# Two attention layers on one core: both value products take their low pass from v's high part alone, placed between transposes of the next probabilities

## The chip, the cores and the metric

The kernel runs on one core of a Trainium2 chip. The metric is device time in microseconds of one execution; of the kernel before there are three runs, with a median of 2325.73 us (2324.55 to 2328.28).

## The reference, cut to what matters

Two layers of gated attention run one after the other over a prompt of 2048 tokens and a sample of 64 tokens (with cached keys and values), model width 1024, 16 heads of 64. Both layers follow the same form:

```
p = rms_norm(x) @ w_in                  # q, k, v, gate
q, k = rms_norm per head
s = q k^T / 8 + bias ; p = softmax(s)   # layer A with a sink per head
o = p v                                 # the value product
y = x + (o * silu(gate)) @ w_out
```

Layer A attends to its own chunk of 64 frames and two before it, with 2 key heads for 16 query heads; layer B to its own chunk and eight before it, each head with its own keys and values.

## The kernel before, in words

**Numbers in two parts.** Operands of products are kept as a high part (rounded to fp32r) and a low part (the rest). A projection tile is made of 8 steps over the model width, each of three products of 512 columns: high by high (L481), high by low (L482), low by high (L483). The value product is made of pairs: `vt`, 128 rows of keys by 128 columns, is the stationary operand, and its columns are v's high part (0 to 63) beside v's low part (64 to 127). The moving operand is the transposed probabilities, first their high part `ph` (or `hi`), then their low part `pl` (or `lo`). The output O has 128 rows in PSUM: 0 to 63 belong to v's high part, 64 to 127 to v's low part; `finish_pairs` (L976 to L985) adds the two halves (two ACT copies L981, two DVE additions L983), multiplies by the gate (POOL, L984) and stores (SP's queue, L985). Every product has a weight load of its own, also where two in a row have the same `vt`.

**Transposes.** The probabilities come out with queries on rows. `transpose` (L597) takes a block of 128 keys as the stationary operand and streams the identity. `split_to` then casts the result from PSUM to the high part (ACT, L569) and subtracts it for the low part (DVE, L570).

**Who sets the order.** On TensorE (PE) the order is written out by hand (`manual_schedule`); ACT, DVE, POOL and the DMA queues are ordered by the framework's own scheduler. The attention steps are mixed with "filler": projection tiles of later units and, after them, the output projections. `filler.to(mark)` puts out projection products until a mark is reached; the marks count projection columns alone.

**Layer A** (`layer_a`, `pipeline` from L941 on) works on items: 4 groups of 4 heads times 17 token tiles (16 of 128 prompt tokens, one of the 64 sample tokens), 68 items. Step i does the scores of item i, filler to 0.3 of the step, `values` of item i-1 (8 transposes, 4 for each of two blocks of keys), filler, `turned` (transposes of queries and of the gate G) at 0.8, and at 0.95 `outputs` of item i-1 (two pairs of 512 columns). The first tile of each group has one block of keys, and the sample item has one block of 128 keys and one of 64.

**Layer B** (`layer_b`, `pipeline` from L1199 on) works on 8 pairs of heads; each goes over 8 units of 256 tokens and the sample unit, which stands between the 7th and the 8th. A step handles one tile and one head: scores, filler, `values` of the step before (up to 5 transposes), then, where a head of a unit has all its tiles transposed, `outputs` of that head one step later, filler. A full output is 6 pairs: 4 of 256 columns and 2 of 128 (L1188 high, L1189 low). For the second head, two transposes of the gate (tile G) stand at the head of `outputs`. The sample unit has 64 query rows: its transposes read 64 rows, its products stream 64 columns, and its third block has 64 keys, so 64 rows of `vt`. `gt`, the transposed gate, has one buffer (L969 to L974).

Of the kernel before, what the change touches and what calls it, by code (L numbers as in the profile page):

```python
# [15 lines left out]
P = 128  # L16
# [35 lines left out]
def hybrid_encoder_kernel(  # L52
# [608 lines left out]
    def layer_a():  # L661
# [243 lines left out]
                op=ALU.mult,  # L905
            )

        def values(it):
            qd = it.qd
            tt, t0, n = it.tile  # L910
            ph = t("ph", [P, 6, 256], 2, F32R)
            pl = t("pl", [P, 6, 256], 2, F32R)
            hi, lo = [], []
            for c, (vt, kn) in enumerate(it.vts):
                PT = psum_a("sa", 512, 4)
                for h in range(4):
                    transpose(PT[:kn, h * n : (h + 1) * n], it.pe[h // 2][:n, h % 2, c * P : c * P + kn])
                hi.append(ph[:kn, 2 * c : 2 * c + 2, :].rearrange("p a b -> p (a b)")[:, : 4 * n])
                lo.append(pl[:kn, 2 * c : 2 * c + 2, :].rearrange("p a b -> p (a b)")[:, : 4 * n])
                bg.anchor(*split_to(hi[c], lo[c], PT[:kn, : 4 * n]))  # L920
            it.hi, it.lo = hi, lo

        def outputs(it):
            qd = it.qd
            tt, t0, n = it.tile
            hi, lo = it.hi, it.lo
            O = psum("o", 512, 1)
            m = len(it.vts)
            for c, (vt, kn) in enumerate(it.vts):
                nc.tensor.matmul(O[:, : 4 * n], vt, hi[c], start=c == 0, stop=False)  # L930
                nc.tensor.matmul(O[:, : 4 * n], vt, lo[c], start=False, stop=c == m - 1)
            finish_pairs(
                O[:, : 4 * n].rearrange("p (j e s) -> p j e s", j=2, e=2),
                it.gt,
                n,
                og[0][:, 2 * qd : 2 * qd + 2, tt * P : tt * P + n],
            )
            key = 0, it.unit[0]
            finished[key] = finished.get(key, 0) + 1

        def pipeline():  # L941
            N = len(items)
            for i in range(-3, N + 1):
                c0 = filler.done
                end = c0 + 5.2
                if i + 3 < N:
                    end = max(items[i + 3].mark, c0 + AVG_A)
                filler.attending = i >= 0
                if 0 <= i < N:
                    scores(items[i])  # L950
                    bg.share(AL, AP_)
                filler.to(c0 + 0.3 * (end - c0))
                if 0 <= i - 1:
                    values(items[i - 1])
                    bg.share(AL, AP_)
                if 0 <= i + 2 < N and items[i + 2].qd == 0:
                    filler.to(c0 + 0.6 * (end - c0))
                    keys(items[i + 2])
                filler.to(c0 + 0.8 * (end - c0))
                turned(items[i + 2] if 0 <= i + 2 < N else None, items[i - 1] if 0 <= i - 1 else None)  # L960
                filler.to(c0 + 0.95 * (end - c0))
                if 0 <= i - 1:
                    outputs(items[i - 1])
                filler.to(end)
                assert i + 3 >= N or items[i + 3].ready

# [21 lines left out]
    def layer_b():  # L988
# [143 lines left out]
                        op=ALU.mult,  # L1132
                    )

        def values(it, i, h):
            u, T, tiles = it.unit
            last = u == NU
            tt, t0, n = tiles[i]
            if i == 0:
                it.ph[h] = t("ph", [P, 6, 256], 2, F32R)  # L1140
                it.pl[h] = t("pl", [P, 6, 256], 2, F32R)
            if last:
                sizes, kb = [P, P, TS], 0
            else:
                kt0 = max(tt - 4, 0)
                sizes, kb = [P] * (tt - kt0 + 1), kt0 - it.base
            PT = psum_b("sb", 1024, 2)
            PTv = PT.rearrange("p (c x) -> p c x", x=P)
            for c, kn in enumerate(sizes):
                transpose(PTv[:kn, c, :n], it.p[i, h][:n, c * P : c * P + kn])  # L1150
            full = sum(kn == P for kn in sizes)
            groups = [(0, full, P)]
            if last:
                groups.append((2, 1, TS))
            for c, m, kn in groups:
                bg.anchor(*split_to(
                    it.ph[h][:kn, kb + c : kb + c + m, t0 : t0 + n],
                    it.pl[h][:kn, kb + c : kb + c + m, t0 : t0 + n],
                    PTv[:kn, c : c + m, :n],
                ))  # L1160
            it.sizes = sizes

        def outputs(it, h):
            u, T, tiles = it.unit
            last = u == NU
            n = tiles[0][2]
            sizes = it.sizes
            if h == 0:
                it.O = psum("o", 512, 1)
            else:  # L1170
                GT = psum("tp", 512, 1)
                for e, (_, t0, _) in enumerate(tiles):
                    transpose(GT[:, t0 : t0 + n], it.G[:n, e * P : (e + 1) * P])
                gt = gate_t(GT[:, :T].rearrange("p (j s) -> p j s", j=1), T)
            mm = []
            if last:
                for c, kn in enumerate(sizes):
                    mm.append((VS[:kn, c, h], c, kn, 0, TS))
            else:
                ta, tb = tiles[0][0], tiles[1][0]  # L1180
                for kt in range(max(tb - 4, 0), ta + 1):
                    mm.append((VT[:, kt, h], kt - it.base, P, 0, UT))
                if ta >= 4:
                    mm.append((VT[:, ta - 4, h], ta - 4 - it.base, P, 0, P))
                mm.append((VT[:, tb, h], tb - it.base, P, P, UT))
            for x, (vt, c, kn, q0, q1_) in enumerate(mm):
                dst = it.O[:, h * T + q0 : h * T + q1_]
                nc.tensor.matmul(dst, vt, it.ph[h][:kn, c, q0:q1_], start=x == 0, stop=False)  # L1188
                nc.tensor.matmul(dst, vt, it.pl[h][:kn, c, q0:q1_], start=False, stop=x == len(mm) - 1)  # L1189
            if h == 1:  # L1190
                finish_pairs(
                    it.O[:, : 2 * T].rearrange("p (j e s) -> p j e s", j=1, e=2),
                    gt,
                    T,
                    og[1][:, it.hp : it.hp + 1, u * UT : u * UT + T],
                )
                finished[1, u] = finished.get((1, u), 0) + 1

        def pipeline():  # L1199
# [9 lines left out]
            for x, it in enumerate(its):  # L1209
                heads = [(i, h) for h in range(2) for i in range(len(it.unit[2]))]  # L1210
                c0 = filler.done
                end, near = c0 + (PACE_B if len(heads) == 4 else PACE_S) * len(heads), 1e9
                if x + 2 < len(its):
                    near = its[x + 2].mark
                    if len(its[x + 1].unit[2]) + len(its[x + 2].unit[2]) < 4:
                        near += MORE
                    end = max(its[x + 2].mark, min(end, its[x + 3].mark - 1.0 if x + 3 < len(its) else end))

                def goal(s):
                    filler.to(c0 + min((end - c0) * s / (2 * len(heads)), (near - c0) * s / NS))  # L1220

                for y, (i, h) in enumerate(heads):
                    scores(it, i, h)
                    bg.share(BL, BP_)
                    goal(2 * y + 1)
                    nxt = None
                    if prev is not None:
                        values(*prev)
                        bg.share(BL, BP_)
                        if prev[1] == len(prev[0].unit[2]) - 1:  # L1230
                            nxt = prev[0], prev[2]
                    prev = it, i, h
                    if pend is not None:
                        outputs(*pend)
                    pend = nxt
                    goal(2 * y + 2)
                    if y == (QY if len(heads) == 4 else QS) and x + 1 < len(its):
                        queries(its[x + 1])
                        near = 1e9
                assert x + 2 >= len(its) or its[x + 2].ready  # L1240
            values(*prev)
            filler.to(filler.done + 2.6)
            if pend is not None:
                outputs(*pend)
            filler.to(filler.done + 2.6)
            outputs(prev[0], prev[2])

        return pipeline

# [175 lines left out]
```

## Time and profile before

| | before |
|---|---|
| median of 3 runs | 2325.73 us (2324.55 to 2328.28) |
| span of the profiled execution, first to last instruction | 2323.8 us |
| median less this span | 1.9 us |
| PE (matmul) busy | 2269.6 us, 98% |
| PE weight loads busy | 1985.2 us, 85% |
| DVE, ACT, POOL busy | 1547.3, 1432.7, 847.6 us |
| mean granted TensorE clock | 0.998 of full speed |

The profiled execution's time is told as its span; what lies around the span is taken as the difference to the median, 1.9 us. PE's busy time is the union of matmul records whose ends are modelled (a product's record goes on while the next one starts), so costs are read from the distance between starts. A weight load's record starts when the load begins, which can be as soon as the product before it has begun to stream; so the start of a load also marks the start of the product before it. A row's form, such as 128\*64 128x256, is rows and columns of the stationary operand and the moving operand's rows by columns.

### The profile page before, as it was taken

To read this page: it belongs to the slowest core of one execution; us is meant where nothing else is said; L and a number is where in the kernel's file an instruction comes from. 1 tells how busy PE (TensorE), PEld (TensorE's weight loads), DVE (VectorE), ACT (ScalarE), POOL (GpSimd) and SP (SyncE) were. 2 spreads that over 40 slices of the span, in tenths; PEclk is the share of its full clock that TensorE was granted. 3 is DMA by queue.
4 is the path that set the end of the run, shared out by engine and by line. 5 is a ranking of instruction groups with operands and counts; after the bars stand their busy time and mean duration, and the time that the engine had idled before them with its cause. 6 is when DMAs were issued, how large, how long until landed. Compare 5 with 4: busy or idle time off the path is not lost.

```text
span 2323.8 us, 42433 instructions
## 1 busy us (share of the span) xinstructions
PE 2269.6 (98%) x13981; PEld 1985.2 (85%) x13981; DVE 1547.3 (67%) x5214; ACT 1432.7 (62%) x3644; POOL 847.6 (36%) x1194
## 2 busy tenths in 40 slices
PE   8899999999999998999999999999999999999999
PEld 7787888888889997878888888888888888888999
DVE  7679988887782228876766767767667677676211
ACT  7778777777772236765665656656656566566321
POOL 5554533333254446432222222222222222224443
PEclk9999999999999999999999999999999999999999
DMA  8846446754446776453444533534435435433664
GB/s 256 263 146 207 162 144 195 229 167 162 134 126 204 226 216 219 145 186 126 158 142 128 161 127 114 178 126 152 143 123 163 134 103 177 131 126 106 189 186 148
DMA packets 232126, 379.37 MB, mean 163 GB/s; under 512 B 24721, under 2 KB 163361, under 8 KB 231873
## 3 DMA queue, kind: packets, MB, share of 16 engines
q1 hardware_dynamic: 231904, 376.65, 51.3%
q8 instruction: 110, 1.80, 0.3%
q14 instruction: 112, 0.91, 0.1%
HBM read 296.13 MB, written 82.08 MB: 163 GB/s over the span
## 4 chain that ended last, share of the span: by engine, by line
PE 77%; DVE 10%; ACT 5%; DMA 5%; issue 2%; POOL 1%; SPq 0%; POOLq 0%; ACTq 0%; DVEq 0%
PE pj L481 13%; PE pj L483 12%; PE pj L482 12%; PE pj L1283 5%; PE pj L1284 5%; PE pj L1285 5%; PE sb L597 5%; PE o L1189 3%; PE o L1188 3%; PE tp L597 3%; PE sb L1110 3%; PE sb L1111 3%; PE sa L597 2%; DVE sq L524 1%; DVE p L1114 1%
## 5 line engine op out<-in xcount | busy, mean ns | idle before, releaser
L481 PE MATMUL pj<-wh,xx 128*128 128x512 f32 (+1 forms) x1648 | 668.7, 406 | 15.2 <-DVE ms L433 7.2
L483 PE MATMUL pj<-wh,xx 128*128 128x512 f32 (+1 forms) x1648 | 638.1, 387 | 0.0
L482 PE MATMUL pj<-wl,xx 128*128 128x512 f32 (+1 forms) x1648 | 635.0, 385 | 0.0
L483 PEld LDWEIGHTS pj<-wh,xx 128*128 128x128 f32 x1648 | 310.4, 188 | 67.3
L481 PEld LDWEIGHTS pj<-wh,xx 128*128 128x128 f32 x1648 | 311.9, 189 | 56.9 <-ACT pb L504 6.5
L386 POOL TENSOR_TENSOR xx<-xraw,xx 128x528 fp32r<-128x528 f32 (+1 forms) x200 | 265.6, 1344 | 218.2 <-ACT xx L385 212.0
L482 PEld LDWEIGHTS pj<-wl,xx 128*128 128x128 f32 x1648 | 312.5, 190 | 37.7
L528 POOL TENSOR_TENSOR f<-f,mhalf 128x4 f32<-128x4 f32 (+3 forms) x221 | 227.9, 1031 | 228.7 <-DVE f L524 216.9
L1118 ACT ACTIVATE p<-p,nm 128x640 f32<-128x640 f32 (+5 forms) x272 | 204.4, 751 | 167.2 <-DVE nm L1114 165.1
L1283 PE MATMUL pj<-xx,wh 128*128 128x264 f32 x1024 | 293.3, 286 | 0.1
L1284 PE MATMUL pj<-xx,wh 128*128 128x264 f32 x1024 | 291.3, 284 | 0.0
L1285 PE MATMUL pj<-xx,wl 128*128 128x264 f32 x1024 | 289.8, 283 | 0.0
L1114 DVE CUSTOM_DVE_ANT_0 p<-sb,BT 128x640 f32<-128x640 f32 (+5 forms) x272 | 196.7, 723 | 119.6 <-PE sb L1111 116.2
L570 DVE TENSOR_TENSOR pl<-sb,ph 128x640 fp32r<-128x640 f32 (+5 forms) x288 | 196.8, 683 | 116.1 <-ACT ph L569 113.7
L385 ACT CAST xx<-xraw 128x528 fp32r<-128x528 f32 (+1 forms) x200 | 123.4, 626 | 220.3 <-PE pj L1285 131.9
L984 POOL TENSOR_TENSOR o<-gt,o 128x256 f32<-128x256 f32 (+2 forms) x140 | 107.4, 767 | 371.3 <-issue 149.0
L569 ACT CAST ph<-sb 128x640 fp32r<-128x640 f32 (+5 forms) x288 | 167.1, 580 | 122.4 <-PE sb L597 114.0
L1288 DVE TENSOR_TENSOR res<-pj,res 128x264 f32<-128x264 f32 x128 | 55.1, 431 | 246.5 <-PE pj L1285 230.7
L1283 PEld LDWEIGHTS pj<-xx,wh 128*128 128x128 f32 x1024 | 192.7, 188 | 0.8 <-DVE res L1288 0.3
L1285 PEld LDWEIGHTS pj<-xx,wl 128*128 128x128 f32 x1024 | 192.6, 188 | 0.0
L1284 PEld LDWEIGHTS pj<-xx,wh 128*128 128x128 f32 x1024 | 192.4, 188 | 0.2
L524 DVE CUSTOM_DVE_ANT_0 sq<-pa 128x64 f32<-128x64 f32 (+1 forms) x850 | 170.2, 253 | 22.1 <-ACT pa L504 20.0
(189 smaller groups left out, 4810.5 us busy)
## 6 DMA issues: line engine op xcount, KB each, us to landing
xx<-xsb SPq DMA_DIRECT2D x224, 512.0 KB, 4.1
xx<-xsa SPq DMA_DIRECT2D x88, 512.0 KB, 4.8
xraw<-oga SPq DMA_DIRECT2D x64, 264.0 KB, 3.4
xraw<-ogb SPq DMA_DIRECT2D x64, 264.0 KB, 3.3
xsa<-xx SPq DMA_DIRECT2D x32, 512.0 KB, 4.0
wraw<-in_w_in_b_dram SPq DMA_DIRECT2D x64, 256.0 KB, 3.4
xsb<-xx SPq DMA_DIRECT2D x32, 512.0 KB, 3.8
xraw<-in_x_dram SPq DMA_DIRECT2D x40, 256.0 KB, 4.1
```

Source lines behind the costliest of these rows:

```text
L386: nc.gpsimd.tensor_tensor(xl, rv, xh.bitcast(F32), op=ALU.subtract)
L481: nc.tensor.matmul(ps[:n, :C], xh, wh, start=k == 0, stop=False)
L482: nc.tensor.matmul(ps[:n, :C], xh, wl, start=False, stop=False)
L483: nc.tensor.matmul(ps[:n, :C], xl, wh, start=False, stop=k == KC - 1)
L528: nc.gpsimd.tensor_tensor(fv, fv, mhalf[:n, :H], op=ALU.pow)
L570: b = nc.vector.tensor_tensor(dst_lo, src, dst_hi.bitcast(F32), op=ALU.subtract)
L597: nc.tensor.transpose(out, in_, ident[:n, :n])
L1114: mi = nc.vector.tensor_tensor_reduce(out=p[:n, :nk], in0=S[:n, o : o + nk], in1=bias[:n, b0 : b0 + nk], op0=ALU.add, op1=ALU.min, scale=1 ...
L1118: ex = nc.scalar.activation(p[:n, :nk], p[:n, :nk], AF.Exp, scale=-1.0, bias=nmh, accum_out=it.sm[:n, 2 * i + h : 2 * i + h + 1],)
L1283: nc.tensor.matmul(ps[:, :OT], wh, oh, start=k == 0, stop=False)
L1284: nc.tensor.matmul(ps[:, :OT], wh, ol, start=False, stop=False)
L1285: nc.tensor.matmul(ps[:, :OT], wl, oh, start=False, stop=k == KC - 1)
```

## The change

`outputs` becomes a generator. It first issues the high product of the first block, then hands a list of low products to its caller, and after that issues the other high products and `finish_pairs`. The low products use the stationary columns 0 to 63 alone (v's high part; blocks of 64 keys keep all columns), so that the product of p's low part with v's low part is left out. `values` takes this list and puts one low product behind each transpose, the rest behind the last. In layer A the low products are cut in two of 256 columns, and `outputs` of item i-2 now stands around `values` of item i-1 at 0.3 of step i; before, it stood at 0.95 of step i-1. In layer B the step stays the same, but `outputs` starts ahead of `values` (with the transposes of G first).

```diff
-        def values(it):
+        def values(it, lows=()):
+            lows = list(lows)
...
                 for h in range(4):
                     transpose(PT[:kn, h * n : (h + 1) * n], it.pe[h // 2][:n, h % 2, c * P : c * P + kn])
+                    if lows:
+                        lows.pop(0)()
...
+            for low in lows:
+                low()
 
         def outputs(it):
...
-            for c, (vt, kn) in enumerate(it.vts):
-                nc.tensor.matmul(O[:, : 4 * n], vt, hi[c], start=c == 0, stop=False)
-                nc.tensor.matmul(O[:, : 4 * n], vt, lo[c], start=False, stop=c == m - 1)
+
+            def high(c):
+                vt, kn = it.vts[c]
+                nc.tensor.matmul(O[:, : 4 * n], vt, hi[c], start=c == 0, stop=c == m - 1 > 0)
+
+            def low(c, q):
+                vt, kn = it.vts[c]
+                M = HD if kn == P and m > 1 else P
+                nc.tensor.matmul(O[:M, q], vt[:, :M], lo[c][:, q], start=False, stop=m == 1)
+
+            high(0)
+            parts = [slice(0, 2 * n), slice(2 * n, 4 * n)] if m > 1 else [slice(0, 4 * n)]
+            yield [lambda c=c, q=q: low(c, q) for c in range(m) for q in parts]
+            for c in range(1, m):
+                high(c)
             finish_pairs(
...
                 filler.to(c0 + 0.3 * (end - c0))
+                out = lows = ()
+                if 0 <= i - 2:
+                    out = outputs(items[i - 2])
+                    lows = next(out)
                 if 0 <= i - 1:
-                    values(items[i - 1])
+                    values(items[i - 1], lows)
+                    for _ in out:
+                        pass
                     bg.share(AL, AP_)
...
                 filler.to(c0 + 0.95 * (end - c0))
-                if 0 <= i - 1:
-                    outputs(items[i - 1])
+                if i == N:
+                    out = outputs(items[i - 1])
+                    for low in next(out):
+                        low()
+                    for _ in out:
+                        pass
...
-        def values(it, i, h):
+        def values(it, i, h, lows=()):
+            lows = list(lows)
...
             for c, kn in enumerate(sizes):
                 transpose(PTv[:kn, c, :n], it.p[i, h][:n, c * P : c * P + kn])
+                if lows:
+                    lows.pop(0)()
...
+            for low in lows:
+                low()
 
         def outputs(it, h):
...
-            for x, (vt, c, kn, q0, q1_) in enumerate(mm):
-                dst = it.O[:, h * T + q0 : h * T + q1_]
-                nc.tensor.matmul(dst, vt, it.ph[h][:kn, c, q0:q1_], start=x == 0, stop=False)
-                nc.tensor.matmul(dst, vt, it.pl[h][:kn, c, q0:q1_], start=False, stop=x == len(mm) - 1)
+            def high(x):
+                vt, c, kn, q0, q1_ = mm[x]
+                nc.tensor.matmul(
+                    it.O[:, h * T + q0 : h * T + q1_], vt, it.ph[h][:kn, c, q0:q1_],
+                    start=x == 0, stop=x == len(mm) - 1,
+                )
+
+            def low(x):
+                vt, c, kn, q0, q1_ = mm[x]
+                M = HD if kn == P else P
+                nc.tensor.matmul(
+                    it.O[:M, h * T + q0 : h * T + q1_], vt[:, :M], it.pl[h][:kn, c, q0:q1_],
+                    start=False, stop=False,
+                )
+
+            high(0)
+            yield [lambda x=x: low(x) for x in range(len(mm))]
+            for x in range(1, len(mm)):
+                high(x)
             if h == 1:
                 finish_pairs(
...
                     nxt = None
+                    if pend is not None:
+                        out = outputs(*pend)
+                        lows = next(out)
+                    else:
+                        out, lows = (), ()
                     if prev is not None:
-                        values(*prev)
+                        values(*prev, lows)
+                        for _ in out:
+                            pass
                         bg.share(BL, BP_)
                         if prev[1] == len(prev[0].unit[2]) - 1:
                             nxt = prev[0], prev[2]
                     prev = it, i, h
-                    if pend is not None:
-                        outputs(*pend)
                     pend = nxt
```

At the end of layer B the last two outputs are issued whole, their low products one behind the other.

## Rows read from the trace of the kernel before

**Rows 1.** Page, part 1, then busy time by stage: layer A, layer B.
```profile
PE 2269.6 (98%) x13981; PEld 1985.2 (85%) x13981; DVE 1547.3 (67%) x5214; ACT 1432.7 (62%) x3644; POOL 847.6 (36%) x1194
...
50.00:720.00 670.00, 652.20 (x3781) 551.88 (x3780) 538.65 (x1953) 504.34 (x1395) 286.66 (x468) 1.00 0.57 179
904.00:2171.00 1267.00, 1248.26 (x7415) 1076.78 (x7415) 887.08 (x2958) 800.40 (x2006) 381.14 (x569) 1.00 0.45 142
```

**Rows 2.** Waits of PE: for what; us in total, times, longest us.
```profile
PE o L931 <- DVE pl L570: 5.9, 11, 1.2
...
PE o L1189 <- DVE pl L570: 2.5, 7, 1.0
...
PE tp L597 <- DVE KB L1071: 1.9, 2, 1.4
```

**Rows 3.** Timeline, layer A: one item's output, its last operation, the next output.
```profile
500.90 0.40 PE L930 MATMUL o<-ph,VT 128*128 128x512 f32 x1
...
501.13 0.39 PE L931 MATMUL o<-pl,VT 128*128 128x512 f32 x1
...
504.93 0.74 POOL L984 TENSOR_TENSOR o<-gt,o 128x256 f32<-128x256 f32 x1 [3.40 <-ACT p L894]
...
509.35 0.39 PE L930 MATMUL o<-ph,VT 128*128 128x512 f32 x1
```

**Rows 4.** Timeline of weight loads in one full output of layer B.
```profile
1501.42 0.19 PEld L1188 LDWEIGHTS o<-ph,VT 128*128 128x128 f32 x1
1501.54 0.19 PEld L1189 LDWEIGHTS o<-pl,VT 128*128 128x128 f32 x1
...
1501.89 0.19 PEld L1188 LDWEIGHTS o<-ph,VT 128*128 128x128 f32 x1
1502.00 0.19 PEld L1189 LDWEIGHTS o<-pl,VT 128*128 128x128 f32 x1
```

**Rows 5.** Timeline of weight loads: four transposes, then products of 64 stationary columns.
```profile
1505.06 0.47 PEld L597 LDWEIGHTS tp<-ident,pa 128*128 128x128 f32 x4
1505.50 0.14 PEld L1110 LDWEIGHTS sb<-KSB,q 128*64 128x64 f32 x1
1505.61 0.14 PEld L1111 LDWEIGHTS sb<-KSB,q 128*64 128x64 f32 x1
1505.67 0.14 PEld L1110 LDWEIGHTS sb<-KSB,q 128*64 128x64 f32 x1
```

**Rows 6.** Weight loads by line and form: busy us, mean ns of one.
```profile
L597 PEld LDWEIGHTS sb<-ident,p 128*128 128x128 f32 x1120 | 135.8, 141 | 47.0 <-issue 7.7 <-DVE pl L570 5.5 <-ACT ph L569 1.9
L1188 PEld LDWEIGHTS o<-ph,VT 128*128 128x128 f32 x672 | 128.1, 191 | 0.6
...
L475 PEld LDWEIGHTS pj<-wl,xx 128*64 128x64 f32 x104 | 14.1, 136 | 3.2
```

**Rows 7.** Tile gt, its reader: count, duration ns min/median/max.
```profile
L984 POOL TENSOR_TENSOR o<-gt,o x140: 319/740/1247, 71.7 to 2170.8; 128x256 f32<-128x256 f32 x128, 128x64 f32<-128x64 f32 x8, 128x128 f32<-128x128 f32 x4
```

**Rows 8.** Timeline, layer B: a low product that waits for its low part.
```profile
1454.13 0.82 DVE L570 TENSOR_TENSOR pl<-sb,ph 128x640 fp32r<-128x640 f32 x1
...
1455.00 0.39 PE L1189 MATMUL o<-pl,VT 128*128 128x256 f32 x1 [0.23 <-DVE pl L570]
```

**Rows 9.** Timeline around the sample's transposes of 64 rows, layer B.
```profile
1509.83 0.39 PE L483 MATMUL pj<-wh,xx 128*128 128x512 f32 x1
...
1510.15 0.23 PEld L597 LDWEIGHTS sb<-ident,p 64*128 64x128 f32 x3 [0.35 <-issue]
1510.47 0.20 PEld L597 LDWEIGHTS tp<-ident,G 128*128 128x128 f32 x2
```

**Rows 10.** Timeline of weight loads: the sample's value products, third block of 64 rows.
```profile
1516.85 0.19 PEld L1188 LDWEIGHTS o<-ph,VS 128*128 128x128 f32 x1
1516.96 0.19 PEld L1189 LDWEIGHTS o<-pl,VS 128*128 128x128 f32 x1
1517.19 0.18 PEld L1188 LDWEIGHTS o<-ph,VS 64*128 64x128 f32 x1
```

More of the change, by code (lines that the diff above doesn't have):

```diff
@@ L1240, in pipeline, with whole @@
                 assert x + 2 >= len(its) or its[x + 2].ready
+            def whole(it, h):
+                out = outputs(it, h)
+                for low in next(out):
+                    low()
+                for _ in out:
+                    pass
             values(*prev)
@@ L1243, in pipeline @@
             if pend is not None:
-                outputs(*pend)
+                whole(*pend)
             filler.to(filler.done + 2.6)
-            outputs(prev[0], prev[2])
+            whole(prev[0], prev[2])
         return pipeline
```

## The prediction

> **What bounds the kernel now.** I read the page's busy times first, then the stages. PE carries a matmul record for 98% of the span; in layer A's stretch it is 652 of 670 us, in layer B's 1248 of 1267, and no other engine passes 81% in either [rows 1]. So an edit counts by what it does to PE's order of work, and other engines count where PE waits for them. Such waits are few: 5.9 us of layer A's low products on the low part of the probabilities, 2.5 us of the same in layer B, 1.9 us of a gate's transposes [rows 2]. Next I took the distances between starts, which give each product's price. A product of 512 columns takes 0.23 us [rows 3], one of 256 takes 0.12, one of 128 with a full stationary operand 0.11 [rows 4]; with 64 stationary columns 128 columns take 0.06 [rows 5]. So the short products with a full operand are bound by their weight load, the long ones by their stream.
>
> **The central question: is a transpose cheaper beside a low product?** The change moves low products between transposes and halves their load. That helps if a transpose is held up by loads. Four transposes load 0.11 apart: the first at 1505.06, the product behind them at 1505.50. That product has 64 stationary columns, whose own load needs at most 0.06 (the pitch of the next two), yet its successor loads only at 1505.61: it began 0.11 after the last transpose, not 0.06 [rows 5]. So what occupies PE for 0.11 is the transpose's stream. The records agree: a transpose's load of 128 columns has 141 ns against 191 for an fp32r one of the same shape and 136 for one of 64 columns [rows 6], as if it were half as long. I conclude that 0.11 is paid per transpose wherever it stands, and that the pair low and transpose costs 0.12 + 0.11 as before.
>
> The Trainium skill, page "TensorE: Matmul & The Clock Gate", section "LDWEIGHTS (loading the stationary operand)", has the load go by columns alone, P / 1.2 ns: 107 ns for 128 columns whatever they are. By that rule the transposes' 0.11 would be their load; the sum would then have the first rival's gain. The trace agrees for fp32r operands (0.11 a product of 128 columns) and not for transposes (141 ns against 191).
>
> **Part by part.**
>
> *Layer A, full items.* Two low products of 512 columns (0.46) become four of 256 (0.47); high products and the eight transposes keep their price. Nothing, within 0.01 us by some 60 items. *Its wait.* The low products now come a step after their cast, so the 5.9 us [rows 2] goes. In the first units PE waits for other things too and part may come back: bounds -6 and 0, taken -5.5.
>
> *Layer A, later finish.* Each item's two ACT copies, two DVE additions, POOL product and store on SP's queue move by 0.35 of a step, behind the casts of the transposes. The store then stands later in SP's queue, ahead of prefetches made a unit early: hidden by that lead. `gt` has one buffer: its next writer (L973) now has half a step, not most of one, after the POOL reader L984 (0.74 us, up to 1.25) [rows 7]. ACT waits behind it at worst; cover is ACT's idle fifth of the stage (504 of 670 us busy [rows 1]). Taken 0, bound +10; not below 0, since nothing is removed.
>
> *Layer B, full outputs.* The two low products of 128 columns load 64 columns: the first falls from 0.11 to 0.06; the second also loads in 0.06, but the full load of the next high product follows it and takes 0.11. So 0.05 saved per output. 14 of the 16 outputs of a pair of heads have it (not the first unit's and second unit's first head, whose short low product is last and is followed by a full load): 112 x 0.05 = -5.6. Bounds -11 (both save) and 0.
>
> *Layer B, an earlier demand.* The first low product stood behind five transposes; now it stands behind one. It needs `pl` four transposes, 0.44 us, earlier. Matching every output's first low product against the end of the subtraction that it needs, I find 17 of 144 that start within 0.11 us of it, and none between 0.11 and 0.74: the slack is used up in 17 and ample in the rest. The pattern is one in which the subtraction ends at 1454.95 and the low product stands until 1455.00 [rows 8]; the 7 waits of rows 2 are those of them whose idle time shows. Of the 17, four in the first pair of heads have fewer transposes to lose. About 13 x 0.4 = +5. Bounds: -2.5 (the scheduler puts the subtraction earlier and the present wait goes) and +7. The gate's two transposes also come earlier, by the 0.54 us of the five they pass; G and the PSUM tile are free long before in all but the two places that wait already, for 1.9 us [rows 2]: nothing, bound +1.
>
> *The sample unit: switches between 64 and 128 rows.* This is the large term. In the trace, PE does not run 64-row and 128-row work back to back. The 512-column product that starts at 1509.83 would end at 1510.06; the sample's 64-row transposes load at 1510.15 and begin one load, 0.06, later: 0.15 lost. Going back to 128 rows, the third of them loads at 1510.27, begins at 1510.33 and ends by 1510.39, and the next loads at 1510.47, beginning at 1510.53: 0.14 lost [rows 9]. Between two short products, which wait for loads anyway, the loss is 0.23 - 0.11 = 0.12 [rows 10]. Now count the switches. The change interleaves 128-row low products with 64-row transposes, and the sample's 64-row low products with 128-row transposes.
> Layer A, per group of heads: `values` of the sample around four low products of the item before: 10 switches instead of 2; the sample's output in the next item's transposes: 6 instead of 2. 12 more x 4 groups = 48, at 0.15: +7.2.
> Layer B, per pair of heads: the sample's first head with the 7th unit's output 6 instead of 2; its second head with the sample's first output 8 instead of 4; the sample's second output in the 8th unit's transposes 4, and 2 around the gate's transpose stay, instead of 4: 10 more. x 8 = 80, at 0.12: +9.6. Against it, four of the sample's low products lose half a load: 4 x 8 x 0.05 = -1.6.
> Together +15.2; bounds +10 (0.08 a switch) and +20 (0.16).
>
> *Sum.* -5.5 - 5.6 + 5 + 15.2 = +9.1, say +10 with a little for what moves to other waits. The profiled execution's 2323.8 becomes about 2334, and with the 1.9 us around it the median 2336.
>
> **Rivals.**
> *Transposes are bound by their load and become cheap between low products.* Some 760 transposes (250 in A, 510 in B) stand ahead of a low product; each would fall from 0.11 to 0.06: -38 on the forecast, 2298. For: the pitch of transposes equals that of load-bound products. Against: [rows 5, 6]. Chance 0.10. The page of the Trainium skill named above speaks for this one.
> *The switches cost nothing between a transpose and a product of 64 stationary columns.* Without the 15 us the sum is -6, 2320. For: the rows show the loss only where full operands or transposes meet, no such pair. Against: it is there with transposes and products on either side [rows 9, 10]. Chance 0.13.
> *`gt`'s single buffer*: L973 stands at the head of ACT until POOL has read, and evacuations of projections behind it come late for PE's two PSUM buffers; from 2 us of wait per item on, ACT's slack is gone. At 0.2 us of PE per item over 60 items +12: 2348. For: from the last product of an output to POOL's end it takes 4.5 us (501.13 to 505.67), half a step of 8.9 [rows 3]. Against: the cover of ACT. Chance 0.11.
> Forecast: 0.66, own range 2327 to 2347.
>
> **How the numbers follow.** A measurement of this kernel tells about 0.2% (4.7 us) from no change, so faster is below 2321.1 and slower above 2330.4. The forecast gives 0.53 slower, 0.12 same, 0.01 faster; the third rival 0.11 slower; the second halves into 0.06 same and 0.07 faster; the first is 0.10 faster. Sum: slower 0.64, same 0.18, faster 0.18. The range 2318 to 2349 takes in the forecast, most of the second rival and half of the third.
>
> **What would show it.** In the changed trace, loads behind a transpose at 0.11 and behind a 256-column low product at 0.12 (right), or transposes at 0.06 (first rival). Around the sample, gaps of 0.2 to 0.3 us between loads, 6 to 10 in each block. No wait of layer A's low products on L570, more of layer B's. Waits of L973 on POOL, and of PE on L504, speak for the third rival. A time below 2321 makes the prediction wrong at the switches or at the transposes; one above 2350 at a wait that I hold to be covered.

## The result and the profile after

The changed kernel takes 2347.09 us (median of 4 runs, 2343.94 to 2348.73) against 2327.01 us of the kernel before in the same comparison (4 runs, 2324.55 to 2330.2): ratio 1.0082, 95% interval 1.0069 to 1.0096. It is slower by some 19 to 20 us where +10 was forecast. The time lies 0.1 us past the forecast's own range (2327 to 2347) and inside the whole one (2318 to 2349). The profiled execution has a span of 2342.1 us.

The page's busy times of the changed kernel, then the stages of layer A and layer B (columns as in [rows 1]):

```profile
PE 2282.7 (97%) x14109; PEld 1999.9 (85%) x14109; DVE 1559.0 (67%) x5214; ACT 1438.6 (61%) x3644; POOL 842.4 (36%) x1194
...
50.00:720.00 670.00, 650.21 (x3856) 555.77 (x3855) 548.34 (x1945) 507.64 (x1392) 281.61 (x467) 1.00 0.56 177
904.00:2171.00 1267.00, 1244.15 (x7301) 1068.33 (x7300) 885.42 (x2954) 800.14 (x2007) 377.73 (x565) 0.99 0.46 141
```

PE is still the bound. Its busy time grew by 13.1 us; that alone decides nothing, since a record goes on while the next product starts. One digit is new: a granted clock of 0.99 in layer B's stretch.

The waits of PE in the changed kernel (us in total, times, longest):

```profile
PE o L1228 <- DVE pl L570: 9.5, 15, 1.6
PE tp L597 <- DVE pa L533: 6.2, 6, 1.5
...
PE sa L877 <- DVE pl L570: 2.1, 3, 1.6
```

Against [rows 2]: layer A's wait of low products is gone, as forecast; layer B's grew from 2.5 to 9.5 us. The waits for `pa` grew from 2.2 us (5 times) to 6.2, and that of the scores (L877) on a subtraction is new.

**Transposes beside low products.** Weight loads of one item of layer A in the changed kernel:

```profile
497.48 0.14 PEld L597 LDWEIGHTS sa<-ident,p 128*128 128x128 f32 x1
497.60 0.14 PEld L942 LDWEIGHTS o<-pl,VT 128*64 128x64 f32 x1
497.71 0.14 PEld L597 LDWEIGHTS sa<-ident,p 128*128 128x128 f32 x1
...
498.17 0.47 PEld L597 LDWEIGHTS sa<-ident,p 128*128 128x128 f32 x4
498.61 0.19 PEld L937 LDWEIGHTS o<-ph,VT 128*128 128x128 f32 x1
```

From the transpose's load (497.48) to the low product's (497.60) 0.12, to the next transpose's 0.11, and the four transposes at the end 0.11 each: a pair costs 0.23 as it did apart.

**The switches.** Weight loads of the sample's first head in layer B, where 64-row transposes and 128-row low products alternate:

```profile
1525.63 0.19 PEld L1220 LDWEIGHTS o<-ph,VT 128*128 128x128 f32 x1
1525.95 0.14 PEld L597 LDWEIGHTS sb<-ident,p 64*128 64x128 f32 x1
1526.15 0.13 PEld L1228 LDWEIGHTS o<-pl,VT 128*64 128x64 f32 x1
1526.41 0.13 PEld L597 LDWEIGHTS sb<-ident,p 64*128 64x128 f32 x1
1526.62 0.13 PEld L1228 LDWEIGHTS o<-pl,VT 128*64 128x64 f32 x1
1526.88 0.11 PEld L597 LDWEIGHTS sb<-ident,p 64*64 64x64 f32 x1
1527.05 0.43 PEld L1228 LDWEIGHTS o<-pl,VT 128*64 128x64 f32 x4
1527.40 0.65 PEld L1220 LDWEIGHTS o<-ph,VT 128*128 128x128 f32 x5
```

Steps of 0.17 to 0.26 at a change of rows, against 0.11 to 0.12 in an item without switches.

**The earlier demand.** TensorE's timeline of an ordinary output of layer B, and the subtraction for which it waits:

```profile
1496.79 0.28 PE L1220 MATMUL o<-ph,VT 128*128 128x256 f32 x1
1496.91 0.27 PE L597 MATMUL sb<-ident,p 128*128 128x128 f32 x1
1497.59 0.33 PE L1228 MATMUL o<-pl,VT 128*64 128x256 f32 x1 [0.40 <-DVE pl L570]
...
1495.96 0.82 DVE L1141 CUSTOM_DVE_ANT_0 p<-sb,BT 128x640 f32<-128x640 f32 x1
...
1496.71 0.82 DVE L570 TENSOR_TENSOR pl<-sb,ph 128x640 fp32r<-128x640 f32 x1
```

DVE comes to the subtraction at 1496.71 and ends it at 1497.53. The low product stands behind one transpose and has nothing to do in the meantime; four transposes and a high product that could run queue behind it.

### The profile page after: what moved, and what is told of

The parts are those of the page before. It is cut to its first block, busy times and chain, and to the rows that moved or that the text cites. A ratio compares the mean times of both kernels' runs of the same rounds, so it can differ in the third digit from the quotient of the medians.

```text
span 2342.1 us, 42555 instructions
## 1 busy us (share of the span) xinstructions
PE 2282.7 (97%) x14109; PEld 1999.9 (85%) x14109; DVE 1559.0 (67%) x5214; ACT 1438.6 (61%) x3644; POOL 842.4 (36%) x1194
## 4 chain that ended last, share of the span: by engine, by line
PE 78%; DVE 9%; DMA 4%; ACT 3%; issue 3%; POOL 2%; SPq 0%; POOLq 0%; DVEq 0%; ACTq 0%
PE pj L481 13%; PE pj L483 12%; PE pj L482 12%; PE sb L597 5%; PE pj L1342 5%; PE pj L1343 5%; PE pj L1344 5%; PE o L1220 3%; PE o L1228 3%; PE tp L597 3%; PE sb L1137 3%; PE sb L1138 3%; PE sa L597 2%; DMA xraw<-in_x_rows_dram 1%; DVE p L1141 1%
## 5 line engine op out<-in xcount | busy, mean ns | idle before, releaser
L1011 POOL TENSOR_TENSOR o<-gt,o 128x256 f32<-128x256 f32 (+2 forms) x140 | 101.8, 727 | 368.9 <-DVE o L1010 107.7
L597 PE MATMUL sb<-ident,p 128*128 128x128 f32 (+2 forms) x1168 | 227.9, 275 | 5.2 <-DVE nm L1141 3.8
```

What stands on the lines that cost most here:

```text
L597: nc.tensor.transpose(out, in_, ident[:n, :n])
```

## Experiments

All ratios are against the kernel before, run on the same chip; 0.001 is 2.3 us. Of 10 kernels, six settle the terms of the sum, two split the change by layer, two try a better order. The changed kernel leaves out the product of the low part of p with the low part of v; so do the runs below in the layers whose low products read 64 columns.

### Without the switches

The changed kernel, with low products kept out of transposes of other rows: in a step whose transposes have 64 rows they stand ahead of them, and the block of 64 keys comes last, behind the high products.

```diff
+            while n < P and lows:
+                lows.pop(0)()
...
-            yield [lambda x=x: low(x) for x in range(len(mm))]
+            yield [lambda x=x: low(x) for x in range(len(mm)) if mm[x][2] == P]
...
+            for x in range(len(mm)):
+                if mm[x][2] < P:
+                    low(x)
```

> The changed kernel, but no low product of 128 rows stands between 64-row transposes (they go ahead of them) and the low products of 64 rows stand behind all high products: the sample unit then has as many switches between 64 and 128 rows as the kernel before; all other outputs stay divided among the transposes. Theory (the switches are the largest term, about 1.8 us for each of four groups of layer A and 0.95 us for each of eight pairs of heads in layer B): about 14 us less than the changed kernel's 2347, so 2331 to 2336. Rival (the loss is in the ordinary outputs, which disturb the transposes or wait for their low part earlier): within 4 us of the changed kernel, 2343 to 2348.

Measured: 2330.95 us (11 runs), ratio 1.0015 (1.0007 to 1.0024). From the changed kernel's 1.0082 that is 0.0067, 15.6 us. The sum has 16.8 for the 128 switches (its +15.2 is less by 1.6 for the sample's half loads, which this run keeps). By the starts of the same projection products in the two traces, the changed kernel loses 1.75 us at the sample of each group of layer A (1.8 expected) and 1.25 us in a pair of heads of layer B (1.2 in the sum). The same sample step, weight loads of this run:

```profile
1518.05 0.19 PEld L1228 LDWEIGHTS o<-ph,VT 128*128 128x128 f32 x1
1518.16 0.73 PEld L1236 LDWEIGHTS o<-pl,VT 128*64 128x64 f32 x6
1518.96 0.23 PEld L597 LDWEIGHTS sb<-ident,p 64*128 64x128 f32 x3
1519.29 0.65 PEld L1228 LDWEIGHTS o<-ph,VT 128*128 128x128 f32 x5
```

From the first high load to the other high loads it takes 1.24 us here, and 1.77 in the changed kernel with 4 switches more: 0.13 a switch.

### Low products whole again, behind the transposes

As the run above, but no low product stands between transposes in either layer; the halved loads stay.

```diff
                     transpose(PT[:kn, h * n : (h + 1) * n], it.pe[h // 2][:n, h % 2, c * P : c * P + kn])
-                    if lows:
-                        lows.pop(0)()
...
                 transpose(PTv[:kn, c, :n], it.p[i, h][:n, c * P : c * P + kn])
-                if lows:
-                    lows.pop(0)()
```

> As the run with the same rows, and in addition the low products are not divided among the transposes: first high product, all transposes, all low products, other high products. Theory (a transpose costs 0.11 us wherever it stands; undivided, the low products of layer B come some 0.44 us later and wait less for their low part): 0 to 7 us less than the run with the same rows, 2325 to 2335. Rival (transposes are cheaper between low products, by 0.05 us for some 700 of them): 30 to 40 us more than the run with the same rows. The transposes' loads stand 0.11 us apart in theory; the low products of 256 columns 0.12.

Measured: 2319.8 us (5 runs), ratio 0.9968 (0.9955 to 0.998), 10.9 us less than the run before it, where the theory had 0 to 7 and its rival 30 to 40 more. The kernel is now faster than the one before, so the interleaving as such gains nothing, and something in it costs 11 us.

### Which layer, and is it the demand or the mixing?

Two more from the run without switches. One takes the low products from between the transposes in layer B alone; the other keeps them at the early place but puts them all ahead of the transposes, so that nothing is mixed.

```diff
                 transpose(PTv[:kn, c, :n], it.p[i, h][:n, c * P : c * P + kn])
-                if lows:
-                    lows.pop(0)()
```

> As the run with the same rows, but in layer B the low products stand behind the step's last transpose; layer A keeps them between its transposes. Theory (the demand is layer B's, the slack used up in 17 outputs there): 2319 to 2324 us, nearly all of the 11 us, and no wait of layer B's low products over 2 us in all. Rival (layer A's divided low products have a share in it, by its waits and its casts): 2325 to 2329 us.

Measured: 2321.24 us (10 runs), ratio 0.9972 (0.9963 to 0.9982). All but 1 us of the 11 is layer B's. Its waits:

```profile
PE o L1234 <- DVE pl L570: 1.8, 2, 1.2
```

9.5 us in 15 waits became 1.8 in 2; both of these lie in the first pair of heads. I compared the two traces projection product by projection product over one pair of heads (that between 1480 and 1635 us). The run with early low products loses 0.42, 0.17 and 0.53 us there in three places, and no other place differs by over 0.05: 1.1 us. Four more pairs show the same three places with 0.15 to 0.17, 0.50 to 0.60 and 0.42 to 0.45 us. The first and the third are outputs that stand for their low part; the second is a step of transposes 3 us ahead of the third. The third in either run, first with early low products, then without:

```profile
1616.21 0.39 PE L1228 MATMUL o<-ph,VT 128*128 128x256 f32 x1
1616.43 0.27 PE L597 MATMUL sb<-ident,p 128*128 128x128 f32 x1
1617.56 0.34 PE L1236 MATMUL o<-pl,VT 128*64 128x256 f32 x1 [0.85 <-DVE pl L570]
```

```profile
1612.00 0.36 PE L1226 MATMUL o<-ph,VT 128*128 128x256 f32 x1
...
1612.58 0.77 PE L597 MATMUL sb<-ident,p 128*128 128x128 f32 x5 [0.21 <-DVE nm L1147]
1613.31 0.81 PE L1234 MATMUL o<-pl,VT 128*64 128x256 f32 x6
```

The early one starts 1.35 us behind its high product, of which only 0.23 are work; the late one starts 1.31 behind it, with all five transposes done. DVE's own order, which the framework's scheduler makes anew for every kernel, has a part in this place: in the late run the subtraction follows the softmax's first pass at once (1612.44), in the early one `pb` and `pa` (L542, L533) stand between (from 1616.16 to the subtraction at 1616.70). No run keeps DVE's order and moves the demand alone. The other run of the two:

```diff
-            while n < P and lows:
+            while lows:
```

> As the run with the same rows (2331 us), but in layer B all low products of an output stand ahead of the step's transposes, none between them. Nothing is interleaved there, and the first low product stands where the change put it or 0.11 us earlier. If the 11 us between that run and the undivided one are the earlier demand on the low part, the time stays or grows: 2330 to 2338 us, and the waits of the low products on the subtraction stay near 9.5 us. If it is the mixing of low products and transposes itself that costs, the time falls towards the undivided run: 2319 to 2326 us.

Measured: 2326.21 us (11 runs), ratio 0.9998 (0.9989 to 1.0007). It falls between the two: 4 us under the run with mixed low products, 6 us over the one with layer B undivided. Both theories had it elsewhere. The waits:

```profile
PE o L1236 <- DVE pl L570: 15.7, 16, 2.1
```

They grew from 9.5 to 15.7 us. Of the growth, 4.0 us lie in the first pair of heads, where in exchange the waits for the softmax (L1147, 3.7 us) are gone; in the pairs behind it, 6.6 us in 11 waits became 8.8 in 11. In the pair compared above this run loses another 0.09, 0.02 and 0.07 us in the same three places. What it gains are steps without a wait, by up to 0.06 each, so that it is 0.13 to 0.24 us shorter net in each of four pairs, and a little clock (below). That is not a price of mixing: at steps without a wait the mixed run and the undivided one are within 0.05 us of each other, either way, and low products ahead of the transposes are shorter than both. So the demand is what costs in layer B. Why low products first are shorter I did not settle.

### Layer A's output a step later, by itself

The kernel before, with layer A's whole output moved to 0.3 of the next step and nothing else changed:

```diff
                 filler.to(c0 + 0.3 * (end - c0))
+                if 0 <= i - 2:
+                    outputs(items[i - 2])
                 if 0 <= i - 1:
...
                 filler.to(c0 + 0.95 * (end - c0))
-                if 0 <= i - 1:
+                if i == N:
                     outputs(items[i - 1])
```

> The kernel before, with layer A's whole output (two pairs of full products, undivided, v's both parts) moved to 0.3 of the next step, ahead of the next item's transposes; layer B as before. Theory: the 5.9 us that the low products waited for their low part go, and come back at the transposes of queries and gate, which then wait for the head norm on DVE: 2325 to 2330. Rival (the later step itself costs, through the single gate buffer or the later finish): 2333 or more, as much as layer A's whole change.

Measured: 2328.05 us (12 runs), ratio 1.0000 (0.9992 to 1.0009). The wait of 5.9 us is gone and the time stays. PE's waits in 50 to 655 us of this run:

```profile
PE tp L597 <- DVE pa L533: 5.1, 3, 3.1
...
PE sa L877 <- DVE pl L570: 2.2, 4, 0.8
PE pj L481 <- DVE pb L509: 2.2, 1, 2.2
```

The kernel before has 2.2, 0 and 0.7 us of these there. At layer A's end comes another, the longest wait from 655 to 720 us in TensorE's timeline of this run:

```profile
671.88 0.59 PE L1285 MATMUL pj<-xx,wh 128*128 128x264 f32 x1 [2.45 <-DVE res L1290]
```

The busy times of 665 to 675 us, first of this run, then of the kernel before:

```profile
665.00:675.00 10.00, 7.55 (x54) 7.30 (x53) 9.71 (x28) 5.91 (x17) 3.92 (x6) 0.84 0.32 97
```

```profile
665.00:675.00 10.00, 10.00 (x85) 9.82 (x84) 9.19 (x27) 5.27 (x17) 2.92 (x6) 1.00 0.23 70
```

From 655 to 675 us DVE is busy for 9.2 to 9.9 of each 10 us in either kernel. The low products had waited for a DVE that was behind; once they no longer do, PE comes sooner to the next thing that DVE owes it.

### Full-width low products

The changed kernel with all 128 stationary columns in every low product, which puts the product of both low parts back.

```diff
-                M = HD if kn == P and m > 1 else P
+                M = P
...
-                M = HD if kn == P else P
+                M = P
```

> The changed kernel with low products of all 128 stationary columns (v's low part is multiplied by p's low part again), everything else in the changed kernel's order. Theory: each full output of layer B loses the 0.05 us of its shorter load (112 outputs, 5.6 us), and some 60 low products of 128 rows that follow 64-row transposes pay a full load of 0.11 instead of 0.06 behind the switch (3 us): 2352 to 2358. Rival (the half load is hidden everywhere): 2345 to 2349.

Measured: 2363.24 us (4 runs), ratio 1.0147 (1.0132 to 1.0162), 15 us over the changed kernel and above the 2352 to 2358 expected: the shorter load is worth more in the changed order than I had said. Compared projection product by projection product over one pair of heads, it is 1.2 to 1.3 us longer: some 0.07 at each of a dozen ordinary outputs, and 0.38 at the sample's three steps. By the starts of the products, an ordinary output loses 0.05 where the second of two short low products meets a full load, as the sum had it, and 4 ns more at each transpose behind a low product (204 ns from start to start for 200, by the median). At the sample a switch costs more with a full load:

```profile
1534.23 0.14 PEld L597 LDWEIGHTS sb<-ident,p 64*128 64x128 f32 x1
1534.44 0.19 PEld L1228 LDWEIGHTS o<-pl,VT 128*128 128x128 f32 x1
1534.75 0.13 PEld L597 LDWEIGHTS sb<-ident,p 64*128 64x128 f32 x1
```

From the low product's load to the 64-row transpose's 0.31, in the changed kernel 0.26. Eight pairs make 10 us; the rest of the 15 lies outside layer B's steady pairs, some of it in the clock (mean 0.9932 of full speed over the runs, 0.9942 in the changed kernel), and is not placed: the profiled execution, at 2357.61 us, is 5.6 shorter than the other three.

### One layer at a time

Layer A as changed with layer B as before, and the reverse; each takes the one layer's functions from the changed kernel and the other's from the kernel before (here the first).

```diff
-        def values(it, i, h, lows=()):
-            lows = list(lows)
+        def values(it, i, h):
...
-                    if pend is not None:
-                        out = outputs(*pend)
-                        lows = next(out)
...
+                    if pend is not None:
+                        outputs(*pend)
```

> Layer A as in the changed kernel, layer B as before. Theory: the changed kernel is some 6 us late at the end of layer A (7 from the sample's switches, the waits saved there given back in part), and layer B adds nothing: 2331 to 2336. Rival (the falls of TensorE's clock in layer B's first pair of heads are started by layer A's later order): 2338 or more, with half clock between 870 and 1030 us.

> Layer A as before, layer B as in the changed kernel. Theory: 12 us of the loss lie in layer B, of which some 7 in its first pair of heads at half clock (1.2 GHz) and the rest in the sample's switches and earlier waits less the shorter low products: 2336 to 2342, with more time at half clock in the first pair of heads than before. Rival (the clock falls because layer A arrives late): 2329 to 2334, half clock no longer than before.

Measured: layer A alone 2338.19 us, ratio 1.0053 (1.004 to 1.0066), above what was expected and in the time range of its rival; layer B alone 2336.33 us, ratio 1.004 (1.0026 to 1.0054), as expected. 0.0053 and 0.0040 add up to the 0.0082 of the change within their intervals. The rival's other sign is missing: between 870 and 1030 us layer A alone has 6.8 us at 1.2 GHz, as the kernel before has; layer B alone has 13.7. Layer A was thought the lesser half and is not: with its wait's 5.5 us given back, its switches (7.0 us in the changed kernel's trace) stand uncovered. The other 5 of its 12.3 us are not settled; its profile has two stretches of 3.4 us at 1.2 GHz near the layer's end, behind waits of 1.24 us for the residual (L1315) and 2.10 us of the last output for the evacuation of the one before it (L1010).

### A better order for the same products

The kernel before with layer B's outputs at their old place, behind the transposes, low products of 64 columns, and the order of the twelve products chosen so that half loads stand beside long streams: high 0, 1, 4, low 0, 1, high 2, 5, low 2, 4, 5, 3, high 3. Layer A is as before.

```diff
+                seq = [(x, 0) for x in long[:2] + short[:1]] + [(x, 1) for x in long[:2]]
+                if len(short) == 2:
+                    seq += [(long[2], 0), (short[1], 0)]
+                seq += [(x, 1) for x in long[2:-1] + short + long[max(2, len(long) - 1):]] + [(long[-1], 0)]
...
+                M = HD if lo and kn == P else P
```

> The kernel before with layer B's outputs in their old place behind all transposes, low products with 64 stationary columns, and an order in which a full load always stands behind a product of 256 columns (high 0, 1, short 4, low 0, 1, high 2, short 5, low 2, 4, 5, 3, high 3); the product of p's low part with v's low part is left out in layer B. Layer A as before. Theory (short products are bound by full loads, 0.11, and fall to 0.06 where the load is hidden): 0.20 us less for 12 outputs of a pair of heads, 0.05 to 0.1 for four, 2.7 per pair, 22 in all, and 2 us of waits less: 2300 to 2309. Rival (what the half load saves was only in the waits): 2319 to 2326.

Measured: 2300.2 us (4 runs), ratio 0.9876 (0.9863 to 0.9889). Weight loads of one full output of this run:

```profile
1492.91 0.42 PEld L1201 LDWEIGHTS o<-ph,VT 128*128 128x128 f32 x3
1493.26 0.19 PEld L1201 LDWEIGHTS o<-pl,VT 128*64 128x64 f32 x2
1493.44 0.30 PEld L1201 LDWEIGHTS o<-ph,VT 128*128 128x128 f32 x2
1493.68 0.38 PEld L1201 LDWEIGHTS o<-pl,VT 128*64 128x64 f32 x4
1493.98 0.19 PEld L1201 LDWEIGHTS o<-ph,VT 128*128 128x128 f32 x1
1494.10 0.19 PEld L481 LDWEIGHTS pj<-wh,xx 128*128 128x128 f32 x1
```

Twelve products in 1.19 us; in the output of which [rows 4] shows a part they take 1.41. A steady pair of heads is 4.3 us shorter, where 2.7 was expected. In five pairs 1.4 us of this lie in one place, the output of [rows 8], against 0.2 at an ordinary one, and the excess is not the loads'. In the kernel before, DVE puts `pa` ahead of the softmax pass (L1114) and stands 0.70 us for POOL; the transposes, and the low product behind them, stand for DVE. First the kernel before, then this run:

```profile
1452.38 0.43 DVE L533 TENSOR_TENSOR pa<-pa,f 128x256 f32<-128x256 f32 x1 [0.70 <-POOL f L528]
1452.72 0.82 DVE L1114 CUSTOM_DVE_ANT_0 p<-sb,BT 128x640 f32<-128x640 f32 x1
...
1453.69 0.74 PE L597 MATMUL sb<-ident,p 128*128 128x128 f32 x5 [0.53 <-DVE nm L1114]
```

```profile
1446.34 0.81 DVE L1114 CUSTOM_DVE_ANT_0 p<-sb,BT 128x640 f32<-128x640 f32 x1
...
1447.11 0.43 DVE L533 TENSOR_TENSOR pa<-pa,f 128x256 f32<-128x256 f32 x1
```

Here the softmax pass stands first and neither wait is left. That order is the framework scheduler's, and the edit did not ask for it. So some 7 of this run's 29 us come with DVE's order (an estimate: 1.2 us in five pairs and 0.7 in the last), and the rest of a pair, 2.9 us, is near the 2.7. Then layer A's high products also ahead of its low ones, operands whole:

```diff
+            rows = [c for c, (_, kn) in enumerate(it.vts) if kn == P]
+            seq = [(c, 0) for c in rows] + [(c, 1) for c in rows]
```

> As the ordered layer B, and in layer A both high products ahead of both low products, so that these ask for their low part 0.23 us later; full stationary operands there and the old place in the step. Theory: of the 5.9 us of waits 2 to 3 go, and half of that comes back at other waits: 0 to 3 us less than the ordered layer B alone.

Measured: 2298.08 us (4 runs), ratio 0.9868 (0.9855 to 0.9881), which beats both kernels. Its 2 us under the run above are within both intervals.

## Why the prediction was right in its direction and short by ten

The steps from the kernel before to the changed one, by the ratios: without interleaving and without switches -7.4 us; the low products between the transposes +10.9; the switches +15.6; together +19.1. The sum had -11.1 (A's wait and the shorter loads), +5 and +15.2. That the time still fell within the range is in part luck: the range reached to 2349 for the sake of the third rival, which did not come true.

- **Transposes cost 0.11 wherever they stand: right.** The changed trace shows the pitch in either place, and the first rival, at 2298 us, fell. The rule of the Trainium skill's page "TensorE: Matmul & The Clock Gate", section "LDWEIGHTS (loading the stationary operand)", by which load time goes with the columns alone, would have given that rival. The trace agrees for fp32r products (0.11 for 128 columns, 0.06 for 64). For transposes it shows that the load does not set the price: 0.11 stays between half loads; how long their load is, only the records of [rows 6] say.
- **The switches, 16.8 of the +15.2: right**, in size (15.6) and in price (0.12 to 0.13 each). The second rival, free switches, fell: a half load beside a transpose changes nothing in kind.
- **"Layer A ... its wait", -5.5: mis-sized; it measured 0** (1.0000, 0.9992 to 1.0009). The prediction allowed for it ("part may come back: bounds -6 and 0") and took the wrong end. The wait's releaser was DVE, near its limit in that stretch; taking a wait for a busy engine away moves it to that engine's next customer: `pa` (L533), the scores (L877), and the residual at the layer's end.
- **"Layer B, an earlier demand", +5, bound +7: mis-sized; it measured 10.0** by the two runs that differ in layer B's place of the low products alone. The places were right, and nearly the price at them: behind the first pair of heads, 11 outputs lose 0.42 to 0.60 us each, 5.4 in all, where about 0.4 was taken. What was missing stands around them. Five steps of transposes ahead of such outputs lose 0.16 each, 0.8. The first pair loses 2.3, about 1 of it by products at 1.2 GHz behind a wait (934 to 936 us). The match of starts against subtractions took the subtraction's end as fixed, while DVE's order changed with the kernel, and steps between waits move too. What is left of the 10 lies within the intervals or is clock (below).
- **Shorter loads, -5.6: within its bounds.** With layer A's wait at 0, the -7.4 of the undivided run is theirs, with what the order of products brings and what DVE's order does. In the traces a steady pair with layer B undivided is 1.7 to 2.0 us shorter than before, 0.7 of it at the output of [rows 8], where waits for DVE shrink; the other 1.0 to 1.2 make 8 to 10 us over eight pairs. The other part is lost ahead of layer B, which the profiled executions with layer A's later output reach 4 to 5 us late (one execution each; over all runs the move of that output by itself costs nothing). In the changed order they are worth more, as the run with full-width low products shows; what each output saves there (0.055) is the 0.05 of the sum.
- **`gt`'s single buffer, the third rival: fell.** The move of layer A's output alone, which carries most of it, costs nothing, and PE's waits for L504 fell from 5.3 to 3.6 us in the changed kernel. (ACT's idle share of that stage, which was to cover it, is a quarter, 166 of 670 us, and not a fifth.)
- **The clock: not foreseen**, and told in the last section.

By place, the changed kernel's profiled execution is some 7 us behind that of the kernel before ahead of layer B (at 860 us) and 14.6 behind at 1060 us, where the first pair of heads is done; then it loses 0.5 to 0.7 us in each of four steady pairs, less than the 0.9 that the sum has for a pair. So the missing ten lie mainly in layer A's wait, which came back, and in layer B's first pair with its waits and clock, and not in the steady pairs.

## What to carry to other kernels

Before a wait is booked as a gain, look at what its releaser does in that stretch: a wait for an engine that is behind came back here at that engine's next readers. Taking work off that engine was not tried. Moving a product into a run of transposes gains nothing where each keeps its price, and it spends slack: at an output without slack the earlier demand cost about the work that it passed (0.42 to 0.60 us for 0.44), and a step ahead of it lost time too. Keep products of 64 and of 128 stationary rows in blocks, since each change between them cost as much here as a short product. And where an edit moves one engine's work, look whether another engine's order has changed with it, before the gain is put down to the edit.

## What was not expected of the hardware

**Switches depend on the load.** A change between 64 and 128 stationary rows shows 0.17 to 0.26 us between loads with a half or a transpose's load, and 0.31 to 0.32 from a full load to a 64-row transpose (0.11 to 0.12 without a change).

**TensorE's clock can fall after it has stood.** In the changed kernel's profile the granted clock is at its lower level, 1.2 GHz, in six places, 23.9 us in all; in the kernel before in three, 11.3 us, the last of them its final microsecond. At each of the six PE had stood, for 1.5 to 2.8 us. Not every such wait does it: after 2.65 us at 30.5 and 1.74 us at 710.9 of the same profile the clock stayed. One of the six, behind layer A's output projections:

```profile
872.85 0.77 PE L481 MATMUL pj<-wh,xx 128*128 128x512 f32 x1 [2.84 <-DVE res L1347]
873.41 0.63 PE L482 MATMUL pj<-wl,xx 128*128 128x512 f32 x1
873.84 0.63 PE L483 MATMUL pj<-wh,xx 128*128 128x512 f32 x1
```

After a wait of 2.84 us the products of 512 columns start 0.43 apart, where they took 0.23 [rows 3]. Over all runs the mean granted clock is 0.9942 in the changed kernel (4 runs), 0.9943 without switches (11), 0.9949 with all low products first (11), 0.9959 with layer B undivided (10), 0.996 undivided (5) and 0.9961 before (15 runs). As an estimate, a difference of 0.0019 over 2347 us is at most about 4.5 us of the 20, and 0.0017 about 4 of the 10.9 between the run without switches and the undivided one; some of that time PE stood and lost nothing by the clock. That a wait costs its own time and then a slower stretch is read from rows; no run isolates it.
